# Rotary with a negative stride on VectorE, and the queries' 1/rms product on POOL as a step of its own

## The chip, the cores and the metric

The kernel runs on one core of a Trainium2 chip. Five engines work side by side, each through its own queue in order: TensorE (PE, with PEld for its weight loads), VectorE (DVE), ScalarE (ACT), GpSimd (POOL) and SyncE (SP), which issues the DMAs. They wait for one another by semaphores. The metric is the device time of one execution in microseconds (us), lower is better.

## The reference

Two layers of an encoder over 512 tokens of width 1024. Each has token heads (12 heads of 64, in 3 groups of 4, one key head for each group), 4 heads that attend to a memory of 256 tokens, an output projection, and a SwiGLU feed-forward part. Layer 0 (mixer A) is banded attention with rotary on the first 16 of a head's 64 elements; layer 1 (mixer B) is global attention in which queries and keys of each head go through an RMS norm and a two-axis rotary first. All is float32. What the change touches:

```python
def apply_rotary(x, cos, sin):
    half = x.shape[-1] // 2
    x1, x2 = xf[..., :half], xf[..., half:]
    return jnp.concatenate([x1 * c - x2 * s, x2 * c + x1 * s], axis=-1)

def mixer_b(q, k, v, qk_g, cos_r, sin_r, cos_c, sin_c):
    q = axial_rope(rms_norm(q, qk_g[0]), cos_r, sin_r, cos_c, sin_c)
    k = axial_rope(rms_norm(k, qk_g[1]), cos_r, sin_r, cos_c, sin_c)
    o = full_attention_blocks(q, k, v)
```

## The kernel before, in words

Tokens lie on the 128 partitions, in 4 tiles. A float32 matmul is made of three with a high and a low part of each operand: a *split* (L276) copies a source into its high part on ScalarE (L280) and subtracts that from the source on VectorE (L284, the low part). Splits of weights (whi, wlo), of queries (q, stored as q2), of probabilities (th, tl) all pass through these two lines.

A mixer makes keys and values first (`kv_pieces`), then the queries in four column groups c = 0 to 3 of four heads each (`q_pieces`; group 3 is the memory heads'), each for the four token tiles t. Below, *tile c.t* is group c, token tile t. A query tile is four pieces of matmul (`prod`, u = 0 to 3) into a PSUM bank with tag "acc" (two buffers). The last piece also takes the result out: ScalarE copies it to qx (L510 in layer 1, L512 in layer 0 and group 3), rotary is put on it, and it is split. Later `stage` turns the split tile on PE (L524) and ScalarE copies it to qT (L525).

`rope_b`, layer 1's rotary with the norm folded in: ScalarE squares (sq, L433); VectorE sums (ss, L434); POOL makes r = (ss/64 + eps) to the power -1/2 (L298, L299); VectorE meanwhile multiplies the two swapped halves with the sine table, one instruction each (rt, L441), x with the cosine table (L442), adds (L443), and multiplies with r (L444). `rope_a`, layer 0's, has no norm and works on 16 elements of each head (L422 to L425).

A head (`heads`) is, for each of four query blocks, a score matmul (L548, L549), its minimum on VectorE (nm, L559), the exponential on ScalarE (p, L560); then 1/denominator on VectorE (rd, L596) and four scalings of p on POOL (L599); then for each of four key blocks j a turn of the probabilities on PE (L609) into a PSUM tile with tag "t" (two buffers, each free again when th and tl have been made from it), the split, and the value matmuls (L623 with th, L624 with tl). After the last, ScalarE and VectorE add the two halves (tmp, L631; tok, L632).

What sets the order: all these steps are put on one time axis by `put` and `lay`, where one unit is one head; `PACE` has the offsets. The steps of queries for later groups so lie between the heads. PE's queue is exactly this order (the framework leaves it alone). In the other engines' queues the framework's scheduler decides when the program is built: it starts from the order in which steps are issued and moves an instruction ahead of others that it reckons to be not yet ready.

Of the kernel before, what the change touches and what calls it, by code (L numbers as in the profile page):

```python
# [23 lines left out]
NG = 3  # L24
NMH = 4
HD = 64
# [153 lines left out]
class Trunk:  # L180
# [246 lines left out]
    def rope_b(self, x, t, n, z):  # L427

        nc = self.nc
        v = nc.vector  # L430
        sq = self.core.tile([P, 4, HD], F32, tag="rt", name="sq", bufs=2)
        ss = self.small.tile([P, 4], F32, tag="ss4", name="ss4", bufs=2)
        nc.scalar.activation(sq[:, :n], x[:, :n], AF.Square)  # L433
        v.tensor_reduce(ss[:, :n], sq[:, :n], axis=AX.X, op=OP.add)  # L434
        r = self.small.tile([P, 4], F32, tag="r4", name="r4", bufs=3)
        self.rstd(r[:, :n], ss[:, :n], HD)
        tmp = self.core.tile([P, 4, HD], F32, tag="rt", name="rt", bufs=2)
        gc, gs = self.gt[:, z, 0, t], self.gt[:, z, 1, t]
        for h in range(2):
            o, i = slice(32 * h, 32 * h + 32), slice(32 - 32 * h, 64 - 32 * h)  # L440
            v.tensor_mul(tmp[:, :n, o], x[:, :n, i], gs[:, None, o].to_broadcast([P, n, 32]))  # L441
        v.tensor_mul(x[:, :n], x[:, :n], gc[:, None, :].to_broadcast([P, n, HD]))  # L442
        v.tensor_add(x[:, :n], x[:, :n], tmp[:, :n])  # L443
        v.tensor_mul(x[:, :n], x[:, :n], r[:, :n, None].to_broadcast([P, n, HD]))  # L444

    def rope(self, l, x, t, n, z):
        (self.rope_b(x, t, n, z) if l else self.rope_a(x, t, n))


    def kv_pieces(self, l):  # L450
        nc = self.nc
        self.ka = self.core.tile([P, NG, S], F32R, name="ka", tag="ka")
        self.kb = self.core.tile([P, NG, S], F32R, name="kb", tag="kb")
        self.vs = self.core.tile([P, NT, NG, P], F32R, name="vs", tag="vs")
        w = self.wkv

        def prod(t, st, u):
            self.ready(t)
            if u == 0:
                st["ps"] = self.tagged("acc" if t < 2 else "s")  # L460
            ps = st["ps"]
            for k in (2 * u, 2 * u + 1):
                c = slice((k % 2) * 384, (k % 2) * 384 + 384)
                self.mm3(ps[:, :384], self.hslice(0, k, t * P, t * P + P), self.hslice(1, k, t * P, t * P + P),
                         w[u][0][:, c], w[u][1][:, c], k == 0, k == KD - 1)
            if u == 3:
                kv = ps[:, :384].rearrange("p (z h d) -> p z h d", z=2, d=HD)
                r = self.rs[:, t:t + 1]
                self.split_scaled(self.vs[:, t, :, :HD], self.vs[:, t, :, HD:], kv[:, 1], r)
                kx = self.core.tile([P, 4, HD], F32, tag="qx", name="kx", bufs=3)  # L470
                ins = nc.scalar.activation(kx[:, :NG], kv[:, 0], AF.Copy, scale=r).ins
# [4 lines left out]
                self.rope(l, kx, t, NG, 1)  # L476
                st["k2"] = self.core.tile([P, 4, 3 * HD], F32R, tag="q2", name="k2", bufs=3)
                self.split(st["k2"][:, :NG, :HD], st["k2"][:, :NG, HD:P], kx[:, :NG])
                self.again(st["k2"][:, :NG])

        out = []
        for t in range(NT):
            st = {}
            out.append(([lambda t=t, st=st, u=u: prod(t, st, u) for u in range(4)],
                        lambda t=t, st=st: self.keys(st["k2"], self.ka, self.kb, t, NG)))
        return out

    def q_pieces(self, l, c, qTs, put, x0, lead):
# [6 lines left out]
        def prod(t, st, u):  # L495
            self.ready(t)
            if c not in qTs:
                qTs[c] = self.core.tile([P, 4, S], F32R, tag="qT", name="qT", bufs=2)
            if u == 0:
                st["ps"] = self.ps.tile([P, 512], F32, tag="acc", name="ps", bufs=2)  # L500
            ps = st["ps"]
            for k in (2 * u, 2 * u + 1):
                cs = slice((k % 4) * 256, (k % 4) * 256 + 256)
                self.mm3(ps[:, :256], self.hslice(0, k, t * P, t * P + P), self.hslice(1, k, t * P, t * P + P),
                         w[k // 4][0][:, cs], w[k // 4][1][:, cs], k == 0, k == KD - 1)
            if u == 3:
                qx = self.core.tile([P, 4, HD], F32, tag="qx", name="qx", bufs=3)
                q = ps[:, :256].rearrange("p (h d) -> p h d", d=HD)
                if l == 1 and c < 3:
                    nc.scalar.activation(qx, q, AF.Copy, scale=self.rs[:, t:t + 1])  # L510
# [17 lines left out]
        for t in range(NT):  # L528
            st = {}
            out.append(([lambda t=t, st=st, u=u: prod(t, st, u) for u in range(4)],  # L530
                        lambda t=t, st=st: stage(t, st)))
        return out


# [114 lines left out]
    def mixer(self, l, mkp, late, tokp):  # L649
# [8 lines left out]
        def put(x, f):  # L658
            bisect.insort(items, (x, next(count), f), key=lambda z: (-z[0], -z[1]))

        def lay(tiles, x0, dx, lag, due):

            for t, (prods, last) in enumerate(tiles):
# [582 lines left out]
```

## Time and profile before

| | |
|---|---|
| runs | 1124.85 us (median of 3; 1124.82 to 1125.47) |
| the profiled execution | 1125.38 us, its span 1123.6 us |
| mixer of layer 0 | about 0 to 140 us |
| mixer of layer 1 | about 560 to 745 us |
| in it, query tiles of group 0 (qx at) | 584.98 to 598.65 us |
| group 1 | 605.02 to 624.98 us |
| group 2 | 633.72 to 661.68 us |

How to read it: rows of a timeline begin with the start (us from the span's beginning) and the duration (us), then the engine, the line, the operation, output<-input with their shapes and how many instructions are merged (x4); brackets give the idle time before and what ended it. Rows of one line give the count and the shortest, middle and longest duration in ns, then the first and last start. Rows of stages give for each engine the busy time in the stage.

### The profile page before, as it was taken

The page shows a single profiled execution, that of the slowest core. Times are in us where ns is not written, and L with a number is a line of the kernel's source. Part 1 is how long each engine was busy: PE and PEld are TensorE (multiplying, and loading weights), DVE is VectorE, ACT ScalarE, POOL GpSimd, SP SyncE. Part 2 cuts the span into 40 slices and gives each one's busy share as a digit, 9 for nine tenths or more (in the row PEclk, how much of TensorE's full clock was granted, in tenths as well). Part 3 has the DMA queues.
Part 4 walks back from the last instruction along what each step waited for, and adds up shares of the span by engine and source line. Part 5 has one row for each costly group of instructions (what it writes and reads, how often), then busy time and mean ns, then how long its engine had stood idle before and what let it go on. Part 6 is the DMA issues. An engine that isn't in the chain of part 4 may idle for free.

```text
span 1123.6 us, 19533 instructions
## 1 busy us (share of the span) xinstructions
PE 1096.6 (98%) x7463; PEld 1003.6 (89%) x7463; DVE 844.3 (75%) x1431; ACT 660.8 (59%) x1343; POOL 203.8 (18%) x348
## 2 busy tenths in 40 slices
PE   8999999999999999999999999999999999999997
PEld 7889988899889989998898888878999899899985
DVE  5688885899557867885788998758996478669854
ACT  6678984666445634663467878756665255345631
POOL 5693331102000000000343543312000000000001
PEclk9999999999999999999999999999999999999999
DMA  6521015443753382325543221145136223423243
GB/s 237 194 81 47 20 57 206 169 132 114 243 180 112 112 283 76 112 79 195 179 150 113 76 76 39 38 150 188 39 113 217 65 76 114 149 62 103 85 166 112
DMA packets 38685, 139.29 MB, mean 124 GB/s; under 512 B 4416, under 2 KB 4800, under 8 KB 38464
## 3 DMA queue, kind: packets, MB, share of 16 engines
q1 hardware_dynamic: 38448, 137.91, 36.4%
q8 instruction: 58, 0.95, 0.3%
q14 instruction: 35, 0.29, 0.1%
q10 hardware_dynamic: 144, 0.14, 0.0%
HBM read 119.16 MB, written 18.87 MB: 123 GB/s over the span
## 4 chain that ended last, share of the span: by engine, by line
PE 68%; DVE 6%; ACT 3%; POOL 2%; issue 2%; DVEq 0%; POOLq 0%; ACTq 0%
PE ps L978 12%; PE ps L979 12%; PE ps L980 12%; PE ps L271 9%; PE ps L270 9%; PE ps L272 9%; PE tp L609 1%; PE o L624 1%; PE o L623 1%; PE s L548 1%; DVE nm L559 1%; PE s L549 1%; DVE wlo L284 1%; POOL r L299 1%; ACT whi L280 1%
## 5 line engine op out<-in xcount | busy, mean ns | idle before, releaser
L280 ACT ACTIVATE whi<-raw 128x1024 fp32r<-128x1024 f32 (+2 forms) x186 | 157.9, 863 | 185.2 <-PE ps L980 81.8
L284 DVE TENSOR_TENSOR wlo<-raw,whi 128x1024 fp32r<-128x1024 f32 (+2 forms) x178 | 175.9, 998 | 74.8 <-ACT whi L280 71.7
L978 PE MATMUL ps<-sf,whi 128*128 128x256 f32 x640 | 179.9, 281 | 0.2
L979 PE MATMUL ps<-sf,wlo 128*128 128x256 f32 x640 | 179.7, 281 | 0.0
L980 PE MATMUL ps<-sf,whi 128*128 128x256 f32 x640 | 179.7, 281 | 0.0
L270 PE MATMUL ps<-whi,f 128*128 128x512 f32 x352 | 137.2, 390 | 0.0
L271 PE MATMUL ps<-wlo,f 128*128 128x512 f32 x352 | 137.1, 390 | 0.0
L272 PE MATMUL ps<-whi,f 128*128 128x512 f32 x352 | 137.0, 389 | 0.0
L980 PE MATMUL ps<-a,whi 128*128 128x256 f32 x480 | 134.4, 280 | 0.0
L978 PE MATMUL ps<-a,whi 128*128 128x256 f32 x480 | 134.3, 280 | 0.0
L979 PE MATMUL ps<-a,wlo 128*128 128x256 f32 x480 | 133.8, 279 | 0.0
L978 PEld LDWEIGHTS ps<-sf,whi 128*128 128x128 f32 x640 | 121.1, 189 | 1.1 <-ACT p L984 0.6
L979 PEld LDWEIGHTS ps<-sf,wlo 128*128 128x128 f32 x640 | 121.4, 190 | 0.5
L980 PEld LDWEIGHTS ps<-sf,whi 128*128 128x128 f32 x640 | 121.4, 190 | 0.0
L308 POOL TENSOR_SCALAR e<-sso 128x1 f32<-128x1 f32 x8 | 3.4, 424 | 566.1 <-ACT junk L303 565.9
L270 PE MATMUL ps<-whi,hT 128*128 128x256 f32 (+1 forms) x320 | 98.8, 309 | 0.9 <-ACT whi L292 0.9
L271 PE MATMUL ps<-wlo,hT 128*128 128x256 f32 (+1 forms) x320 | 93.9, 294 | 2.6 <-DVE wlo L284 1.9
L599 POOL TENSOR_SCALAR p<-p,rd 128x256 f32<-128x256 f32 (+2 forms) x128 | 78.2, 630 | 99.8 <-DVE rd L596 50.3
L272 PE MATMUL ps<-whi,hT 128*128 128x256 f32 (+1 forms) x320 | 93.7, 293 | 0.0
L979 PEld LDWEIGHTS ps<-a,wlo 128*128 128x128 f32 x480 | 90.5, 188 | 0.2
L978 PEld LDWEIGHTS ps<-a,whi 128*128 128x128 f32 x480 | 90.4, 188 | 0.2
L980 PEld LDWEIGHTS ps<-a,whi 128*128 128x128 f32 x480 | 90.1, 188 | 0.0
(201 smaller groups left out, 2735.0 us busy)
## 6 DMA issues: line engine op xcount, KB each, us to landing
raw<-in_wgu_dram SPq DMA_DIRECT2D x48, 512.0 KB, 4.4
raw<-in_wd_dram SPq DMA_DIRECT2D x44, 512.0 KB, 4.4
rb<-in_wgu_dram SPq DMA_DIRECT2D x40, 512.0 KB, 3.6
raw<-in_wo_dram SPq DMA_DIRECT2D x17, 512.0 KB, 3.6
raw<-in_wq_dram SPq DMA_DIRECT2D x16, 512.0 KB, 5.0
xt<-x SPq DMA_DIRECT2D x12, 512.0 KB, 4.5
raw<-in_wm_dram SPq DMA_DIRECT2D x8, 512.0 KB, 4.3
x<-y SPq DMA_DIRECT2D x8, 512.0 KB, 3.0
```

Of the source, the lines that this page charges most:

```text
L270: mm(out, lh, rh, start=first, stop=False)
L271: mm(out, lh, rl, start=False, stop=False)
L272: mm(out, ll, rh, start=False, stop=last)
L280: nc.scalar.activation(hi, src, AF.Copy)
L284: nc.vector.tensor_sub(lo, src, hi.bitcast(F32))
L299: g.tensor_tensor(r, r, self.mhalf[:, :r.shape[1]], op=OP.pow)
L548: nc.tensor.matmul(s[:, :n], qi, hd["ka"]()[:, k0 * P:k1 * P], start=True, stop=False)
L549: nc.tensor.matmul(s[:, :n], qi, hd["kb"]()[:, k0 * P:k1 * P], start=False, stop=True)
L599: self.pooled = nc.gpsimd.tensor_scalar(hd["p"][z][:, :n], hd["p"][z][:, :n], rd[:, z:z + 1], 1.0, op0=OP.mult, op1=OP.mult)
L978: mm(out, wh[:, s], rh, start=start and k == 0, stop=False, skip_group_check=True)
L979: mm(out, wl[:, s], rh, start=False, stop=False, skip_group_check=True)
L980: mm(out, wh[:, s], rl, start=False, stop=k == 3, skip_group_check=True)
```

## The change

The two multiplications of the swapped halves become one in both ropes: x is read as (heads, 2 halves, half length) with the axis of the halves running backwards. `rope_b` no longer multiplies with r; it returns it. For keys the product follows at once, on VectorE as before. For queries the product goes to POOL, and product and split become a step of their own (`parts`), which `lay` puts 0.15 after the end of the tile's pieces (x0 + (t + 1) dx), where the split was part of the last piece (x0 + (t + 0.75) dx). In layer 0 and group 3 there is no r, and `parts` is the split alone.

```diff
+    def halves(self, x):
+        return x.rearrange("p n (h d) -> p n h d", h=2)
...
-        v.tensor_mul(tmp[:, :n, 0:8], x[:, :n, 8:16], sn[:, None, 0:8].to_broadcast([P, n, 8]))
-        v.tensor_mul(tmp[:, :n, 8:16], x[:, :n, 0:8], sn[:, None, 8:16].to_broadcast([P, n, 8]))
+        v.tensor_mul(self.halves(tmp[:, :n]), self.halves(x[:, :n, 0:16])[:, :, ::-1],
+                     self.halves(sn[:, None, :].to_broadcast([P, n, 16])))
...
-        for h in range(2):
-            o, i = slice(32 * h, 32 * h + 32), slice(32 - 32 * h, 64 - 32 * h)
-            v.tensor_mul(tmp[:, :n, o], x[:, :n, i], gs[:, None, o].to_broadcast([P, n, 32]))
+        v.tensor_mul(self.halves(tmp[:, :n]), self.halves(x[:, :n])[:, :, ::-1],
+                     self.halves(gs[:, None, :].to_broadcast([P, n, HD])))
         v.tensor_mul(x[:, :n], x[:, :n], gc[:, None, :].to_broadcast([P, n, HD]))
         v.tensor_add(x[:, :n], x[:, :n], tmp[:, :n])
-        v.tensor_mul(x[:, :n], x[:, :n], r[:, :n, None].to_broadcast([P, n, HD]))
+        return r
...
+                st["qx"], st["r"] = qx, None
                 if c < 3:
-                    self.rope(l, qx, t, 4, 0)
-                st["q2"] = self.core.tile([P, 4, 3 * HD], F32R, tag="q2", name="q2", bufs=3)
-                self.split(st["q2"][:, :, :HD], st["q2"][:, :, HD:P], qx)
+                    st["r"] = self.rope(l, qx, t, 4, 0)
+
+        def parts(st):
+            qx, r = st["qx"], st["r"]
+            if r is not None:
+                nc.gpsimd.tensor_tensor(qx, qx, r[:, :, None].to_broadcast([P, 4, HD]), op=OP.mult)
+            st["q2"] = self.core.tile([P, 4, 3 * HD], F32R, tag="q2", name="q2", bufs=3)
+            self.split(st["q2"][:, :, :HD], st["q2"][:, :, HD:P], qx)
...
+                for f in mid:
+                    put(min(x0 + (t + 1) * dx + 0.15, due(t) - 0.002), f)
```

PE's queue and SP's are the same before and after. Line numbers shift: in the rows of the changed kernel the product is L524, L437 is the sum of squares (L434 before), L442 the swapped halves (L441), L444 and L445 the cosine product and the sum (L442 and L443), L514 and L436 are qx and sq (L510 and L433), L535 is qT (L525), L569 and L570 are nm and p (L559 and L560), L606 is rd (L596), L609 the scaling of p (L599), L641 and L642 are tmp and tok (L631 and L632).

POOL's queue before, for tiles 2.0 and 2.1 (r_7950 and r_8079 are their 1/rms, ss their sums of squares, p the probabilities of the head in hand):

```order
L298 TENSOR_SCALAR r_7950<-ss_7947 128x4
L299 TENSOR_TENSOR r_7950<-r_7950,mhalf 128x4
L599 TENSOR_SCALAR p<-p,rd 128x512 x4
L298 TENSOR_SCALAR r_8079<-ss_8076 128x4
L299 TENSOR_TENSOR r_8079<-r_8079,mhalf 128x4
```

And POOL's queue in the changed kernel, from the same place (r_7922 and r_8050 belong to tiles 2.0 and 2.1):

```order
L298 TENSOR_SCALAR r_7922<-ss_7919 128x4
L299 TENSOR_TENSOR r_7922<-r_7922,mhalf 128x4
L609 TENSOR_SCALAR p<-p,rd 128x512 x4
L524 TENSOR_TENSOR qx<-qx,r_7922 128x256
L298 TENSOR_SCALAR r_8050<-ss_8047 128x4
L299 TENSOR_TENSOR r_8050<-r_8050,mhalf 128x4
L609 TENSOR_SCALAR p<-p,rd 128x512 x4
L524 TENSOR_TENSOR qx<-qx,r_8050 128x256
```

The product stands behind the four scalings. It stands so in tiles 1.1, 1.3 and 2.0 to 2.3; in group 0 and in tiles 1.0 and 1.2 it stands right behind the root.

ScalarE's queue before, around the split of tile 2.1 (q_8088 is its high part, th the high parts of turned probabilities):

```order
L510 ACTIVATE qx<-ps,rs 128x256
L433 ACTIVATE sq<-qx 128x256
L560 ACTIVATE p,den<-s,nm 128x512
L280 ACTIVATE th<-tp 128x512
L631 ACTIVATE tmp<-o 64x512
L525 ACTIVATE qT<-tp 128x4x128
L280 ACTIVATE q_8088<-qx 128x4x64
L280 ACTIVATE th<-tp 128x512
L560 ACTIVATE p,den<-s,nm 128x512
L280 ACTIVATE th<-tp 128x512
```

And in the changed kernel:

```order
L514 ACTIVATE qx<-ps,rs 128x256
L436 ACTIVATE sq<-qx 128x256
L570 ACTIVATE p,den<-s,nm 128x512
L280 ACTIVATE th<-tp 128x512
L641 ACTIVATE tmp<-o 64x512
L535 ACTIVATE qT<-tp 128x4x128
L570 ACTIVATE p,den<-s,nm 128x512
L280 ACTIVATE q_8088<-qx 128x4x64
L280 ACTIVATE th<-tp 128x512 x2
L570 ACTIVATE p,den<-s,nm 128x512
```

The split now stands one exponential later, and still ahead of both th; it waits for POOL where it waited for VectorE. In tiles 1.3 and 2.0 it stands ahead of qT and th, in tile 1.1 ahead of the next tile's qx.

VectorE's queue before, for the same tile (tl is the low part of turned probabilities):

```order
L443 TENSOR_TENSOR qx<-qx,rt 128x256
L284 TENSOR_TENSOR tl<-tp,th 128x512
L444 TENSOR_TENSOR qx<-qx,r_8079 128x256
L559 TENSOR_REDUCE nm<-s 128x1
L632 TENSOR_TENSOR tok<-o,tmp 64x512
L284 TENSOR_TENSOR q_8088<-qx,q_8088 128x4x64
L284 TENSOR_TENSOR tl<-tp,th 128x512
L559 TENSOR_REDUCE nm<-s 128x1
```

And in the changed kernel, from the swapped halves on:

```order
L442 TENSOR_TENSOR rt<-qx,gt 128x256
L437 TENSOR_REDUCE ss_8047<-sq 128x4
L444 TENSOR_TENSOR qx<-qx,gt 128x256
L606 RECIPROCAL rd<-den 128x4
L445 TENSOR_TENSOR qx<-qx,rt 128x256
L284 TENSOR_TENSOR tl<-tp,th 128x512
L569 TENSOR_REDUCE nm<-s 128x1
L642 TENSOR_TENSOR tok<-o,tmp 64x512
L569 TENSOR_REDUCE nm<-s 128x1
L284 TENSOR_TENSOR q_8088<-qx,q_8088 128x4x64
L284 TENSOR_TENSOR tl<-tp,th 128x512 x2
```

The product with r is gone from VectorE; the low part of the split stands one minimum later, ahead of two tl.

More of the change, by code (lines that the diff above doesn't have):

```diff
@@ L438, in rope_b @@
         gc, gs = self.gt[:, z, 0, t], self.gt[:, z, 1, t]
-        for h in range(2):
-            o, i = slice(32 * h, 32 * h + 32), slice(32 - 32 * h, 64 - 32 * h)
-            v.tensor_mul(tmp[:, :n, o], x[:, :n, i], gs[:, None, o].to_broadcast([P, n, 32]))
+        v.tensor_mul(self.halves(tmp[:, :n]), self.halves(x[:, :n])[:, :, ::-1],
+                     self.halves(gs[:, None, :].to_broadcast([P, n, HD])))
         v.tensor_mul(x[:, :n], x[:, :n], gc[:, None, :].to_broadcast([P, n, HD]))
         v.tensor_add(x[:, :n], x[:, :n], tmp[:, :n])
-        v.tensor_mul(x[:, :n], x[:, :n], r[:, :n, None].to_broadcast([P, n, HD]))
+        return r
     def rope(self, l, x, t, n, z):
-        (self.rope_b(x, t, n, z) if l else self.rope_a(x, t, n))
+        return self.rope_b(x, t, n, z) if l else self.rope_a(x, t, n)
     def kv_pieces(self, l):
@@ L475, in prod @@
                         nc.sync.dma_start(self.mT[:, z, ks].bitcast(F32), self.spill[:, z, ks])
-                self.rope(l, kx, t, NG, 1)
+                r = self.rope(l, kx, t, NG, 1)
+                if l:
+                    nc.vector.tensor_mul(kx[:, :NG], kx[:, :NG], r[:, :NG, None].to_broadcast([P, NG, HD]))
                 st["k2"] = self.core.tile([P, 4, 3 * HD], F32R, tag="q2", name="k2", bufs=3)
@@ L530, in q_pieces @@
             out.append(([lambda t=t, st=st, u=u: prod(t, st, u) for u in range(4)],
-                        lambda t=t, st=st: stage(t, st)))
+                        lambda t=t, st=st: stage(t, st), lambda st=st: parts(st)))
         return out
@@ L661, in lay @@
         def lay(tiles, x0, dx, lag, due):
-            for t, (prods, last) in enumerate(tiles):
+            for t, (prods, last, *mid) in enumerate(tiles):
                 for u, f in enumerate(prods):
                     put(x0 + (t + u / len(prods)) * dx, f)
+                for f in mid:
+                    put(min(x0 + (t + 1) * dx + 0.15, due(t) - 0.002), f)
                 put(min(x0 + (t + 1) * dx + lag, due(t) - 0.001), last)
```

## The prediction

> **What bounds the kernel now.** I read the page first: span, busy shares, and the shares of the chain that ended last.
>
> ```profile
> span 1123.6 us, 19533 instructions
> PE 1096.6 (98%) x7463; PEld 1003.6 (89%) x7463; DVE 844.3 (75%) x1431; ACT 660.8 (59%) x1343; POOL 203.8 (18%) x348
> PE 68%; DVE 6%; ACT 3%; POOL 2%; issue 2%; DVEq 0%; POOLq 0%; ACTq 0%
> ```
>
> TensorE is the bound: it stands still for 1123.6 - 1096.6 = 27 us. The change touches the mixers alone, so the next view is the busy time of each engine by stage: layer 1's first queries (585 to 600), its heads of groups 0 to 2 (600 to 668), and layer 0's heads.
>
> ```profile
> core 0: us, PE busy (x) PEld busy (x) DVE busy (x) ACT busy (x) POOL busy (x), PEclk, DMA share, GB/s
> 585.00:600.00 15.00, 13.14 (x98) 11.94 (x98) 11.73 (x31) 8.27 (x20) 5.14 (x7) 1.00 0.06 13
> 600.00:632.00 32.00, 31.49 (x226) 28.16 (x225) 28.06 (x65) 25.50 (x60) 16.95 (x24) 1.00 0.45 160
> 632.00:668.00 36.00, 34.48 (x235) 29.89 (x235) 34.26 (x68) 28.92 (x68) 17.76 (x24) 1.00 0.17 59
> 43.00:112.00 69.00, 66.56 (x525) 63.26 (x523) 55.61 (x172) 51.20 (x142) 41.75 (x66) 1.00 0.26 86
> ```
>
> From 632 to 668 VectorE is 95% busy (34.26 of 36) while PE idles 1.5 us; at 600 to 632 PE idles 0.5, at 585 to 600 1.9. So **all that a lighter VectorE can win in layer 1 is some 3 us**: 1.5 + 0.5 + about 1.1, the one stall at 585 to 600 that VectorE's own queue makes (quoted below). The clock is granted in full.
>
> **The change part by part.** First, prices.
>
> ```profile
> L441 DVE TENSOR_TENSOR rt<-qx,gt x24: 275/282/432, 585.5 to 663.0; 128x128 f32<-128x128 f32 x24
> L442 DVE TENSOR_TENSOR qx<-qx,gt x12: 406/418/426, 586.4 to 663.3; 128x256 f32<-128x256 f32 x12
> L444 DVE TENSOR_TENSOR qx<-qx,r x12: 408/426/885, 588.2 to 664.7; 128x256 f32<-128x256 f32 x12
> L643 POOL TENSOR_TENSOR gt<-ru x2: 734/1225/1716, 275.1 to 275.8; 128x256 f32<-128x256 f32 x2
> ...
> 275.08 2.42 POOL L643 TENSOR_TENSOR gt<-ru 128x256 f32<-128x256 f32 x2
> 275.26 1.64 DVE L284 TENSOR_TENSOR wlo<-rb,whi 128x1024 fp32r<-128x1024 f32 x1
> ```
>
> (1) **The swapped halves.** Two instructions of 0.28 become one of 256 elements. No row shows a negative stride. Lower end 0.42, as L442 with as many elements; upper end 0.84, twice that, as if it streamed at half the rate. I take 0.42, the nearest row: VectorE gains 0.14 in each of 12 tiles, and in layer 0, where such instructions are shorter still, no more. In layer 0 nothing waits on it (55.6 of 69 us busy), so I take 0 there, with 1 us either way for the splits that move. Where the sum of squares stood between the two halves, it now stands behind the whole: 0.14 later. At 0.84 it would be another 0.42 later.
>
> The Trainium skill's Vector Engine (DVE) Microarchitecture Reference, section 5.1, lists how the engine streams an operand with a negative step among the things not measured; the bounds above do without it.
>
> (2) **The product on POOL.** Twelve times 0.43 leave VectorE (0.86 where POOL scales probabilities beside it) and twelve products come to POOL. The nearest row is L643: the same engine, operation and size, one operand repeated. It took 0.73 and 1.72. I take 0.73, since the long one, from 275.8, ran beside a VectorE instruction with two operands in SBUF, and beside the new product VectorE reads PSUM or waits; 1.72 stays as the upper end. By itself it costs nothing: POOL is 18% busy.
>
> The Trainium skill's GPSIMD Engine Reference, section 3, speaks against the move: elementwise work belongs on VectorE, and it measures a two-input add at 1.96 times VectorE's time. By that the product would take 0.43 x 1.96, an estimate of 0.83, and the sum below would be 6 x 0.1 = 0.6 us higher; L643 over L444, 734 to 426, is 1.7 times.
>
> (3) **Where the product stands.** This decides. Tile 2.1 as it ran, from the timelines of POOL, ScalarE, VectorE and TensorE:
>
> ```profile
> 644.67 0.19 POOL L298 TENSOR_SCALAR r<-ss 128x4 f32<-128x4 f32 x1 [5.16 <-DVE ss L434]
> 644.95 1.17 POOL L299 TENSOR_TENSOR r<-r,mhalf 128x4 f32<-128x4 f32 x1
> 646.11 3.27 POOL L599 TENSOR_SCALAR p<-p,rd 128x512 f32<-128x512 f32 x4
> 647.11 0.42 ACT L280 ACTIVATE q<-qx 128x256 fp32r<-128x256 f32 x1
> 647.43 0.58 ACT L280 ACTIVATE th<-tp 128x512 fp32r<-128x512 f32 x1
> 646.22 0.86 DVE L444 TENSOR_TENSOR qx<-qx,r 128x256 f32<-128x256 f32 x1
> 648.75 0.67 DVE L284 TENSOR_TENSOR tl<-tp,th 128x512 fp32r<-128x512 f32 x1
> 649.48 0.66 PE L609 MATMUL tp<-cst,p 128*128 128x128 f32 x4
> ```
>
> VectorE could multiply at 646.22, as soon as POOL had the root. In the changed queue (shown with the change) the product stands behind the four scalings of the head in hand, on an engine that works in order. The scalings took 2.87 us at the least (a row below). So the product ends at 646.11 + 0.15 (late sum of squares) + 2.87 + 0.73 = 649.86, where ScalarE began the split at 647.11. The split stands in ScalarE's queue ahead of the two th, and its other half stands in VectorE's ahead of the two tl; **all behind it wait**. Then q and th: 649.86 + 0.32 + 0.58 = 650.76; tl ends 0.67 later at 651.43. The next turn of probabilities on PE (L609) needs the PSUM buffer that this tl frees: it went at 649.48 and now goes at 651.5, 2.0 us late, with PE idle before it. What follows on PE, up to the next tile's qx, is issued behind it, so the next round starts late too: the slips add.
>
> The other five tiles with the scalings between root and product, their scalings on POOL and then what waits on PE:
>
> ```profile
> 614.34 3.05 POOL L599 TENSOR_SCALAR p<-p,rd 128x512 f32<-128x512 f32 x4
> 628.31 3.23 POOL L599 TENSOR_SCALAR p<-p,rd 128x512 f32<-128x512 f32 x4
> 636.65 2.87 POOL L599 TENSOR_SCALAR p<-p,rd 128x512 f32<-128x512 f32 x4
> 655.01 2.87 POOL L599 TENSOR_SCALAR p<-p,rd 128x512 f32<-128x512 f32 x4
> 664.59 3.31 POOL L599 TENSOR_SCALAR p<-p,rd 128x512 f32<-128x512 f32 x4
> 617.53 0.36 PE L270 MATMUL ps<-whi,hT 128*128 128x256 f32 x1
> 632.29 0.40 PE L624 MATMUL o<-tl,vs 128*128 128x512 f32 x1
> 641.75 0.40 PE L624 MATMUL o<-tl,vs 128*128 128x512 f32 x1
> 658.93 0.66 PE L609 MATMUL tp<-cst,p 128*128 128x128 f32 x4 [0.63 <-DVE tl L284]
> 668.08 0.60 PE L609 MATMUL tp<-cst,p 128*128 128x128 f32 x4
> 638.99 0.59 ACT L525 ACTIVATE qT<-tp 128x512 fp32r<-128x512 f32 x1
> 639.47 0.59 ACT L280 ACTIVATE th<-tp 128x512 fp32r<-128x512 f32 x1
> 616.04 0.48 ACT L510 ACTIVATE qx<-ps,rs 128x256 f32<-128x256 f32 x1 [0.24 <-PE ps L272]
> ```
>
> - Tile 2.2: 655.01 + 0.15 + 3.60 = 658.76; q, th, tl as above (1.57): 660.33 for 658.93, **1.4**.
> - Tile 2.3: 664.59 + 0.15 + 3.60 + 1.57 = 669.91 for 668.08, **1.8**.
> - Tile 2.0: here qT stands between q and th (0.48, from 638.99 to 639.47): 636.65 + 0.15 + 3.60 + 0.32 + 0.48 + 0.58 + 0.67 = 642.45; the value product L624 waits for this tl, 641.75 before: **0.7**.
> - Tile 1.3: the same without the 0.15 (both halves stood ahead of the sum): 633.96 for 632.29, **1.7**.
> - Tile 1.1: product done at 614.34 + 3.60 = 617.94; the split stands ahead of the next tile's qx (616.04 before), which now starts at 618.26 and ends at 618.74. Its accumulator is the one that PE's L270 at 617.53 takes over: **1.2**.
>
> Tiles 1.0 and 1.2 have the product straight behind the root and the wait is short: 0. Sum with 2.0 for tile 2.1: 2.0 + 1.4 + 1.8 + 0.7 + 1.7 + 1.2 = **8.8 us**.
>
> (4) **Group 0 of layer 1**, where no head runs yet.
>
> ```profile
> 593.50 0.50 PE L524 MATMUL tp<-identr,q 128*128 128x128 f32 x4 [0.48 <-DVE q L284]
> 597.43 0.39 PE L271 MATMUL ps<-wlo,hT 128*128 128x256 f32 x1 [1.13 <-DVE wlo L284]
> ```
>
> The product is 0.73 - 0.43 longer, the merge 0.14 shorter: each of the first two splits comes some 0.2 later, and PE waits for it. Then wlo no longer queues behind a product that waits for the root, and the 1.13 goes. But tile 0.2's product now meets that wlo, and ScalarE comes late to its exponentials. I take 0, with -1 to +1.
>
> All DMA issues keep their place on SP, and PE's order is unchanged, so no transfer moves by more than these slips. After 668 nothing makes them up: PE, 98% busy over the span, is in order and carries them to the end. Sum: the profiled execution took 1125.38, its span 1123.6 and 1.8 around it; + 8.8 gives 1134.2. Against the median of the runs, 1124.85, 0.5 lower: 1133.7. **I predict 1134.**
>
> **The rivals.**
>
> *Faster: the lighter VectorE decides.* From 632 to 668 it was the fullest engine after PE, and it loses 0.86 + 0.14 a tile and the slowed half of the split. If ScalarE came to the split only after the product had ended, all 3 us of idle PE might go: 1121.8. The point from which it decides: the product must end where ScalarE reaches it, about 647.8 in tile 2.1 (one exponential, 0.7, now stands ahead of the split that began at 647.11), so 2 us earlier than reckoned. Against it: root and scalings alone end at 649.1. **0.11.**
>
> *Nothing changes: the wait replaces waits that were there.*
>
> ```profile
> 659.86 0.69 ACT L560 ACTIVATE p<-s,nm 128x512 f32<-128x512 f32 x1 [1.79 <-DVE nm L559]
> ```
>
> ScalarE idled anyway behind these instructions for VectorE's minima, here 1.8 us; if PE's buffers give as much room, the slip is 0 to 0.3 a tile: 1125 to 1127. Against it: L609 already waited for tl at 649.48 and 658.93, so there is no room. Nor does the change fail to do what it says: each tile's swap is one instruction in the new queue. **0.11.**
>
> *Slower still: the product at its upper end.* 1.72 for 0.73 adds 1.0 in six tiles, and 1 in group 0: 1141. **0.10.** The swap at 0.84 adds 6 x 0.42 = 2.5, and stays inside my forecast's own range.
>
> **How the numbers follow.** My forecast, slips of 4 to 14 us, has 0.68: 1129 to 1139. From 1124.5 to 1141 lie the forecast, the upper price and about half of "nothing", 0.83 together, so that is the range. A measurement of this kernel tells about 0.2% (2.2 us) from no change. Faster by over that 0.11, within 0.10, slower 0.79 (a slip of 0.3 a tile ends just outside).
>
> **What would show it.**
>
> ```profile
> 643.18 0.47 ACT L510 ACTIVATE qx<-ps,rs 128x256 f32<-128x256 f32 x1
> 652.10 0.46 ACT L510 ACTIVATE qx<-ps,rs 128x256 f32<-128x256 f32 x1
> ```
>
> Right: ScalarE's q waits about 2 us for POOL in six tiles of layer 1; L609 and L624 on PE idle for tl there; from one qx to the next of group 2 pass 10 to 11 us, here 8.92; VectorE's share at 632 to 668 falls while the stage grows; everything before 585 and the FFN are as long as before. Wrong: q finds its operand ready, the POOL product is over 1.5 us or the swap over 0.6, or the time moves in layer 0.

## The result, and the profile after

The changed kernel took **1134.16 us** (median of 4 executions, 1133.92 to 1134.17), the one before 1124.84 (1124.79 to 1125.47) beside it: a ratio of 1.0081, 95% interval 1.0064 to 1.0099. Put on another chip among the experiments it took 1132.99 (1.0079, 1.0065 to 1.0093). The forecast was 1134, with 1124.5 to 1141 as its range. Among the experiments one execution of the kernel before ran at a granted clock of 0.56 and took 1795 us; no comparison counts it.

The page of the profile after: the span, the busy time of each engine, and the chain that ended last.

```profile
span 1132.4 us, 19488 instructions
PE 1099.4 (97%) x7463; PEld 1005.6 (89%) x7463; DVE 834.4 (74%) x1387; ACT 660.7 (58%) x1343; POOL 207.2 (18%) x360
PE 66%; DVE 5%; POOL 3%; ACT 3%; issue 2%; DMA 1%; POOLq 0%; DVEq 0%; ACTq 0%
```

VectorE has 10 us less work than before and POOL 3 more, as the change says. TensorE's idle time grew by 6 us, to 33, and its busy time by 2.8, though it runs the same 7463 instructions. That second number needs an explanation of its own; it comes below.

The prices, from the views of the two lines (least, median and most ns of one):

```profile
L442 DVE TENSOR_TENSOR rt<-qx,gt x12: 410/416/427, 585.2 to 669.4; 128x256 f32<-128x256 f32 x12
L524 POOL TENSOR_TENSOR qx<-qx,r x12: 612/614/730, 587.7 to 674.5; 128x256 f32<-128x256 f32 x12
```

Tile 2.1, the one that the prediction worked through: POOL, ScalarE, VectorE and TensorE in turn. In square brackets is how long the engine stood idle before the row, and what ended that.

```profile
648.98 2.71 POOL L609 TENSOR_SCALAR p<-p,rd 128x512 f32<-128x512 f32 x4
651.65 0.62 POOL L524 TENSOR_TENSOR qx<-qx,r 128x256 f32<-128x256 f32 x1
652.30 0.42 ACT L280 ACTIVATE q<-qx 128x256 fp32r<-128x256 f32 x1 [2.15 <-POOL qx L524]
652.62 1.07 ACT L280 ACTIVATE th<-tp 128x512 fp32r<-128x512 f32 x2
653.23 1.29 DVE L284 TENSOR_TENSOR tl<-tp,th 128x512 fp32r<-128x512 f32 x2
654.07 0.63 PE L619 MATMUL tp<-cst,p 128*128 128x128 f32 x4 [3.28 <-DVE tl L284]
```

Read it from the bottom: PE stands for 3.28 us, until VectorE has made a tl; the tl needs a th; both th stand in ScalarE's queue behind q; q stands 2.15 us, until POOL's product is done; the product stands behind four scalings that have nothing to do with it. Two of ScalarE's instructions were ready and could not pass the one that wasn't. TensorE's other waits of that kind, from its timeline (tiles 1.1, 2.0, 2.2 and 2.3):

```profile
621.99 0.63 PE L619 MATMUL tp<-cst,p 128*128 128x128 f32 x4 [1.36 <-DVE tl L284]
...
644.69 0.51 PE L634 MATMUL o<-tl,vs 128*128 128x512 f32 x1 [0.23 <-DVE tl L284]
...
664.95 0.63 PE L619 MATMUL tp<-cst,p 128*128 128x128 f32 x4 [2.07 <-DVE tl L284]
...
676.87 0.63 PE L619 MATMUL tp<-cst,p 128*128 128x128 f32 x4 [1.52 <-DVE tl L284]
```

Tile 1.3 has no such wait, though its q stood 1.92 us for POOL. The value product that takes the low part queued behind this q (a PE instruction that multiplies tl with the values) had 1.84 us of room before. Here are the tl and the product before; then q, the tl and the product after:

```profile
631.41 0.67 DVE L284 TENSOR_TENSOR tl<-tp,th 128x512 fp32r<-128x512 f32 x1
633.92 0.40 PE L624 MATMUL o<-tl,vs 128*128 128x512 f32 x1
...
632.74 0.42 ACT L280 ACTIVATE q<-qx 128x256 fp32r<-128x256 f32 x1 [1.92 <-POOL qx L524]
634.17 0.69 DVE L284 TENSOR_TENSOR tl<-tp,th 128x512 fp32r<-128x512 f32 x1
635.10 0.39 PE L634 MATMUL o<-tl,vs 128*128 128x512 f32 x1
```

The tl ends at 634.86, 2.8 us later than before, and the product starts at 635.10, 1.2 later, as late as PE was already: the room took up the wait.

The same stage by its rhythm: the first qx of layer 1, those of group 2, and the first of group 3 (line 516).

```profile
584.08 0.46 ACT L514 ACTIVATE qx<-ps,rs 128x256 f32<-128x256 f32 x1
...
636.17 0.47 ACT L514 ACTIVATE qx<-ps,rs 128x256 f32<-128x256 f32 x1
...
645.94 0.47 ACT L514 ACTIVATE qx<-ps,rs 128x256 f32<-128x256 f32 x1
...
656.61 0.47 ACT L514 ACTIVATE qx<-ps,rs 128x256 f32<-128x256 f32 x1
...
667.91 0.47 ACT L514 ACTIVATE qx<-ps,rs 128x256 f32<-128x256 f32 x1 [0.32 <-PE ps L272]
...
679.40 0.47 ACT L516 ACTIVATE qx<-ps,rq 128x256 f32<-128x256 f32 x1
```

From one qx of group 2 to the next pass 9.8, 10.7 and 11.3 us. From 584.08 to 679.40 are 95.32 us; before, the same stretch (584.98 to 670.66) took 85.68. So the loss of 9.3 lies here, 9.64 by this measure. After it the changed kernel stays 8.3 to 8.8 us behind, up to the end. The busy time by stage says so from another side: from 632 to 676 VectorE is now busy for 31.0 us of 44 (70%, where it was 95%), and PE is idle for 6.3.

The last view is one that the prediction didn't ask for again after it had found the clock granted in full: 1 us windows, with TensorE's granted clock in the column PEclk.

```profile
core 0: us, PE busy (x) PEld busy (x) DVE busy (x) ACT busy (x) POOL busy (x), PEclk, DMA share, GB/s
666.00:667.00 1.00, 1.00 (x6) 0.87 (x5) 0.92 (x2) 0.41 (x2) 0.00 (x0) 0.65 0.06 16
667.00:668.00 1.00, 1.00 (x6) 1.00 (x5) 0.37 (x1) 0.68 (x3) 0.00 (x0) 0.50 0.00 0
668.00:669.00 1.00, 1.00 (x4) 0.71 (x4) 0.24 (x1) 0.80 (x2) 0.00 (x0) 0.50 0.45 74
669.00:670.00 1.00, 1.00 (x7) 0.80 (x6) 1.00 (x3) 0.51 (x1) 0.00 (x0) 0.65 0.93 266
```

For 3.4 us, from 666.3 to 669.7, the clock was granted at half, 1.4 us after the end of PE's second long stop. A matmul of 256 columns takes 0.42 there in place of 0.28. The price is the missing share: 0.35 + 0.50 + 0.50 + 0.35 = **1.7 us** on PE; set beside the same instructions before, PE goes into the stretch 6.02 us late and comes out 7.58 late. It explains more than half of the growth in PE's busy time. How much of it the end of the kernel keeps is reckoned below.

### The profile page after: what moved, and what is told of

The parts are those of the page before. It is cut to its first block, busy times and chain, and to the rows that moved or that the text cites. A ratio compares the mean times of both kernels' runs of the same rounds, so it can differ in the third digit from the quotient of the medians.

```text
span 1132.4 us, 19488 instructions
## 1 busy us (share of the span) xinstructions
PE 1099.4 (97%) x7463; PEld 1005.6 (89%) x7463; DVE 834.4 (74%) x1387; ACT 660.7 (58%) x1343; POOL 207.2 (18%) x360
## 4 chain that ended last, share of the span: by engine, by line
PE 66%; DVE 5%; POOL 3%; ACT 3%; issue 2%; DMA 1%; POOLq 0%; DVEq 0%; ACTq 0%
PE ps L990 12%; PE ps L992 12%; PE ps L991 12%; PE ps L271 9%; PE ps L270 9%; PE ps L272 9%; POOL p L609 1%; PE tp L619 1%; PE o L634 1%; DVE wlo L284 1%; PE o L633 1%; POOL r L299 1%; DMA pair<-whi 1%; POOL qx L524 1%; PE s L558 1%
## 5 line engine op out<-in xcount | busy, mean ns | idle before, releaser
L609 POOL TENSOR_SCALAR p<-p,rd 128x256 f32<-128x256 f32 (+2 forms) x128 | 74.4, 600 | 101.6 <-DVE rd L606 46.5
```

The source lines that it names most:

```text
L609: self.pooled = nc.gpsimd.tensor_scalar(hd["p"][z][:, :n], hd["p"][z][:, :n], rd[:, z:z + 1], 1.0, op0=OP.mult, op1=OP.mult)
```

## The experiments

Four theories were held against each other. **A**, the prediction's: the product waits behind four scalings on POOL, and the split that waits for it blocks what is queued behind it on ScalarE and VectorE. **B**: what costs is the product on POOL as such, its 0.61 us and what it takes from VectorE beside it, wherever it stands. **C**: the merged swap with its negative stride. **D**: the split's own, later step. Each run is compared with runs of the kernel before on its own chip.

### The product back on VectorE, all else as changed

```diff
-                nc.gpsimd.tensor_tensor(qx, qx, r[:, :, None].to_broadcast([P, 4, HD]), op=OP.mult)
+                nc.vector.tensor_mul(qx, qx, r[:, :, None].to_broadcast([P, 4, HD]))
```

> The changed kernel with one edit: the queries' product with 1/rms goes back from POOL to VectorE; the merged swap and the split's own step stay. Theory A (on POOL the product stands behind four scalings of 2.7 us, and the split that waits for it blocks ScalarE and VectorE): the wait goes, so 1123 to 1126 us, q on ScalarE waits under 0.3 us in the tiles of group 2, and qx to qx there is 8.9 to 9.3 us. Theory C (the merged swap with its negative stride costs the time) and theory D (the split's own later step costs it): both parts are still here, so 1132 to 1135.

Measured: **1122.52 us**, ratio 0.9984 (0.9975 to 0.9993). This is 0.5 below A's range. Tile 2.1 in its timelines, VectorE's product and ScalarE's q:

```profile
645.68 0.43 DVE L524 TENSOR_TENSOR qx<-qx,r 128x256 f32<-128x256 f32 x1 [0.27 <-POOL r L299]
646.28 0.41 ACT L280 ACTIVATE q<-qx 128x256 fp32r<-128x256 f32 x1
```

VectorE takes the product 0.03 us after the root is there; q waits for nobody, and the longest wait of PE for a tl that is left in group 2 is 0.31. The whole loss is gone, and slightly more, with merged swap and own step in place: C and D fall. (qx to qx in group 2 is 8.6 to 9.2 here.)

### The merged swap alone

The product is back on VectorE and the split back in the same step as the swap; only the merge is left. Three dots mark what is left out of an edit; here it is the rest of the step's own function, which goes.

```diff
                 if c < 3:
-                    st["r"] = self.rope(l, qx, t, 4, 0)
-
-        def parts(st):
...
+                    r = self.rope(l, qx, t, 4, 0)
+                    if r is not None:
+                        nc.vector.tensor_mul(qx, qx, r[:, :, None].to_broadcast([P, 4, HD]))
+                st["q2"] = self.core.tile([P, 4, 3 * HD], F32R, tag="q2", name="q2", bufs=3)
+                self.split(st["q2"][:, :, :HD], st["q2"][:, :, HD:P], qx)
```

> Only the merged swap is left of the change; product on VectorE and the split in the same step as before the change. Theory A: no loss, 1123.5 to 1125.5 us (the one instruction took 0.42 us for the two of 0.28, on an engine that seldom sets the pace). Theory C: 1132 to 1135. Theory D: as A here; it is told apart by the difference to the run with the product on VectorE.

Measured: **1123.34 us**, 0.9991 (0.9982 to 1.0), 0.2 below A's range. A swap of 0.42 for two of 0.28 wins at most 0.2%, and loses nothing. With the split's own step (1122.52) it is no slower.

### The product on POOL, issued early

The product goes into the step of the swap; the split keeps its own. The order of POOL's queue changes by that: in tiles 1.3 and 2.0 to 2.3 the product now comes behind the first of the four scalings, in tile 1.1 still behind all four.

```diff
                 if c < 3:
-                    st["r"] = self.rope(l, qx, t, 4, 0)
+                    r = self.rope(l, qx, t, 4, 0)
+                    if r is not None:
+                        nc.gpsimd.tensor_tensor(qx, qx, r[:, :, None].to_broadcast([P, 4, HD]), op=OP.mult)
...
         def parts(st):
             qx, r = st["qx"], st["r"]
-            if r is not None:
-                nc.gpsimd.tensor_tensor(qx, qx, r[:, :, None].to_broadcast([P, 4, HD]), op=OP.mult)
```

> The product stays on POOL but is issued in the same step as the swap, so that in tiles 1.3 and 2.0 to 2.3 it stands behind one scaling and not four; in tile 1.1 still behind four. The split keeps its step. Theory A: the product ends about 2 us earlier in those tiles, but ScalarE also comes to q about 1 us earlier (before the copy of qT and an exponential), so about 1 us of wait stays in each of the four tiles of group 2: 1127 to 1131 us, between the two kernels. Theory B (what costs is the time of a product on POOL, its own 0.61 us and what it takes from VectorE by running beside it, wherever it stands): 1133 to 1136, as all twelve products are still on POOL.

Measured: **1127.68 us**, 1.0029 (1.0018 to 1.0041). POOL, ScalarE and PE in tile 2.1 (POOL's product is line 521 here):

```profile
645.80 0.69 POOL L609 TENSOR_SCALAR p<-p,rd 128x512 f32<-128x512 f32 x1
646.46 0.61 POOL L521 TENSOR_TENSOR qx<-qx,r 128x256 f32<-128x256 f32 x1
647.11 0.42 ACT L280 ACTIVATE q<-qx 128x256 fp32r<-128x256 f32 x1 [1.31 <-POOL qx L521]
650.17 0.63 PE L619 MATMUL tp<-cst,p 128*128 128x128 f32 x4 [1.46 <-DVE tl L284]
```

The product ends 2 us sooner after the root, but ScalarE now reaches q before the copy of qT and an exponential, and stands 1.31 us for it. Between the two kernels, as A said, and not what B asked for: twelve products on POOL, of the same length, at 5 to 6 us less.

### Early product, late split

As the last one, and in layer 1 the split's step comes later, so that ScalarE has a th ahead of q.

```diff
-                    put(min(x0 + (t + 1) * dx + 0.15, due(t) - 0.002), f)
+                    put(min(x0 + (t + 1) * dx + (0.45 if l else 0.15), due(t) - 0.002), f)
```

> As the run with the early product, and in layer 1 the split's step comes later (0.45 of a head behind the tile instead of 0.15): on ScalarE q then stands behind the first of the two high parts th (group 2) or behind both (group 1). Theory A: q finds its operand ready in tiles 1.3 and 2.0 to 2.3 (wait under 0.3 us) and only tile 1.1 can wait; 1123 to 1126 us. Theory B: 1133 to 1136, as all twelve products are still on POOL. Theory D (a later split costs by itself): over 1134.

Measured: **1122.85 us**, 0.9987 (0.9978 to 0.9996), 0.15 below A's range. Tile 2.1, and the one wait of more than 0.75 us that PE has left in the stage (tile 1.1's):

```profile
645.53 0.69 POOL L609 TENSOR_SCALAR p<-p,rd 128x512 f32<-128x512 f32 x1
646.20 0.60 POOL L521 TENSOR_TENSOR qx<-qx,r 128x256 f32<-128x256 f32 x1
647.31 0.43 ACT L280 ACTIVATE q<-qx 128x256 fp32r<-128x256 f32 x1
620.78 0.63 PE L619 MATMUL tp<-cst,p 128*128 128x128 f32 x4 [1.35 <-DVE tl L284]
```

The product is done at 646.80, ScalarE takes q at 647.31 without a wait. Twelve products on POOL cost nothing where they stand well: **B falls**. What is lost in the changed kernel is lost by two places in two queues.

### Only the split later

The product stands behind four scalings as in the changed kernel; the edit is the one number of the last diff.

> The changed kernel with one number changed: in layer 1 the split's step comes 0.45 of a head behind the tile instead of 0.15. On POOL the product still stands behind four scalings in six tiles; on ScalarE q now stands behind the first high part th, ahead of the second (group 2), or behind the copy of qT and both th (group 1). Theory A (the harm is what stands behind the waiting q): the product ends as late as in the changed kernel, q waits still (1 to 1.6 us), but only the second th stands behind it: about half of the loss goes, 1127 to 1131 us. Theory B (a late product on POOL and its own time cost, whatever is queued behind): 1133 to 1134.

Measured: **1126.31 us**, 1.0015 (1.0006 to 1.0024), somewhat below the range that A gave. ScalarE and PE in tile 2.1, where POOL's product ends at 649.93:

```profile
649.97 0.42 ACT L280 ACTIVATE q<-qx 128x256 fp32r<-128x256 f32 x1 [1.65 <-POOL qx L524]
649.19 0.63 PE L619 MATMUL tp<-cst,p 128*128 128x128 f32 x4 [0.71 <-DVE tl L284]
```

ScalarE still stands for 1.65 us, but one th has passed q, and PE goes on 0.8 us *before* q even starts. Of the 10.2 us between the changed kernel and the run with VectorE's product (8.5 above the kernel before and 1.7 below it) 3.7 are left, so two thirds are gone, not half: PE stands 0.71 us in this tile where it stood 3.28, and without the long stops the clock stayed up throughout the stage (worth up to 1.7 of it). A wait is as dear as what is queued behind it.

### No product at all

In layer 1 the queries' product with 1/rms is left out.

```diff
-            if r is not None:
-                nc.gpsimd.tensor_tensor(qx, qx, r[:, :, None].to_broadcast([P, 4, HD]), op=OP.mult)
```

> The changed kernel without the queries' product with 1/rms in layer 1 (this part of the computation is left out); the root of the mean square is still taken, the four scalings and the split's own step stay. It shows what is to be had at most from taking the product off both engines. Theory A and the first step of the prediction (some 3 us in all): no wait for POOL, 1120.5 to 1123.5 us. If the split's own step cost by itself (theory D): over 1130. If the lighter VectorE gave much more than step 1 reckoned: under 1119.5.

Measured: **1119.66 us**, 0.9958 (0.9944 to 0.9971), a little below the range. ScalarE's first q of layer 1, from its timeline, and the window of group 0 (PE's busy time stands behind the length):

```profile
586.17 0.42 ACT L280 ACTIVATE q<-qx 128x256 fp32r<-128x256 f32 x1 [1.50 <-DVE qx L445]
```

```profile
584.00:600.00 16.00, 16.00 (x121) 15.00 (x121) 12.44 (x29) 9.69 (x22) 6.44 (x10) 1.00 0.33 100
```

The surplus comes from group 0: without the product no split waits for the root, q waits 1.50 us where it waited 2.38 before, and PE has no gap at all from 584 to 600, where it idled for 1.9 us from 585 to 600. So 4.7 us (1124.37 less 1119.66) is what can be won at most by taking this product off both engines; the prediction's 3 us counted VectorE's load and left out the wait for the root.

### A dose: the product twice

In groups 1 and 2 the product is issued twice, one behind the other (the queries are multiplied by 1/rms twice).

```diff
                 nc.gpsimd.tensor_tensor(qx, qx, r[:, :, None].to_broadcast([P, 4, HD]), op=OP.mult)
+                if c:
+                    nc.gpsimd.tensor_tensor(qx, qx, r[:, :, None].to_broadcast([P, 4, HD]), op=OP.mult)
```

> The changed kernel with the product issued twice in groups 1 and 2, one behind the other on POOL (the queries are multiplied by 1/rms twice): a dose of the product's price. Theory A: in tile 1.3 and in 2.0 to 2.3 the whole 0.61 us of the second one comes onto the path, 3.0 together, and up to 1 us more in tiles 1.1 and 1.2, against 1133.4 of the changed kernel: 1135.5 to 1138 us; qx to qx in group 2 grows by about 0.6. If the product's length is hidden (the scalings alone set the wait): 1133 to 1134.

Measured: **1141.72 us**, 1.015 (1.0136 to 1.0164): 3.7 us above the range that A gave. A miss in size, and a useful one. The second product's line, PE's longest wait in its timeline, and the granted clock in five windows:

```profile
L526 POOL TENSOR_TENSOR qx<-qx,r x8: 612/612/615, 608.4 to 681.2; 128x256 f32<-128x256 f32 x8
```

```profile
657.44 1.09 PE L621 MATMUL tp<-cst,p 128*128 128x128 f32 x4 [3.94 <-DVE tl L284]
```

```profile
657.00:658.00 1.00, 0.56 (x3) 0.59 (x4) 0.89 (x2) 0.72 (x3) 0.00 (x0) 0.64 0.00 0
660.00:661.00 1.00, 1.00 (x7) 0.97 (x6) 0.70 (x2) 0.78 (x2) 0.00 (x0) 0.66 0.00 0
674.00:675.00 1.00, 1.00 (x5) 0.82 (x5) 0.19 (x1) 0.76 (x2) 0.00 (x0) 0.83 0.13 25
687.00:688.00 1.00, 1.00 (x4) 0.78 (x3) 0.31 (x1) 0.72 (x2) 0.00 (x0) 0.50 0.00 0
688.00:689.00 1.00, 1.00 (x10) 0.91 (x9) 0.71 (x2) 0.59 (x1) 0.00 (x0) 1.00 0.00 0
```

The first turn of probabilities after the wait takes 1.09 us for four, where it took 0.63. Behind each of the three waits of 3.94, 2.75 and 2.71 us in group 2 the clock is halved, up to 660.7, 674.3 and 688.0 (a mean of 0.66 from 660 to 661 is half clock until 660.68). Three stretches for the changed kernel's one are some 3.3 us, which is about the miss. The other 5.4 of the 8.7 us over the changed kernel's 1133 come near the five products of 0.61 that A counted, 3.0, and a new wait of 2.15 us on ScalarE in tile 1.2, whose product now stands behind four scalings too. This is a sum, not shown by a run with the same waits and the clock kept up.

### The loss split by place

Two halves of the change, and the changed kernel itself, on one chip: the products of group 2 alone on POOL (the others on VectorE), and those of groups 0 and 1 alone.

```diff
-            if r is not None:
+            if r is not None and c == 2:
                 nc.gpsimd.tensor_tensor(qx, qx, r[:, :, None].to_broadcast([P, 4, HD]), op=OP.mult)
+            elif r is not None:
+                nc.vector.tensor_mul(qx, qx, r[:, :, None].to_broadcast([P, 4, HD]))
```

The other half has `c < 2`.

> The changed kernel with the products of groups 0 and 1 on VectorE again; those of group 2 stay on POOL, behind four scalings each. It splits the loss by place. From the traces of the changed kernel and of the run with all products on VectorE, set at the same first qx of layer 1 (584.1): up to the first qx of group 2 the changed kernel falls 2.9 us behind (636.17 against 633.30), from there to the end of group 2 another 7.6 (679.40 against 668.95), and 1.7 of those are a stretch of 3.4 us at half the granted clock (666.3 to 669.7) behind TensorE's idle time. Theory A, the slips add: 1122.5 + 7.6 = 1130 us with one such stretch, 1128.4 with none; 1127.5 to 1131. If the slips do not add, so that PE makes up in group 2 what group 1 lost: 1133.

> The other half: the products of groups 0 and 1 on POOL as in the changed kernel, those of group 2 on VectorE. Theory A: 1122.5 + 2.9 = 1125.4 us, 1124.5 to 1126.5, no stretch at half clock, qx to qx in group 2 8.6 to 9.2 us.

> The changed kernel itself, once more beside the two halves on the same chip: 1133 to 1134.5 us; by theory A the two halves' losses against the run with all products on VectorE (1122.5) add up to this one's, within 1.7 us, the price of one stretch at half clock.

Measured, against the kernel before: group 2 alone **1131.27 us**, 1.0057 (1.0045 to 1.007); groups 0 and 1 alone **1125.14**, 1.0006 (0.9997 to 1.0015); both **1132.99**, 1.0079. Group 2's time is 0.3 above A's range, the others are in theirs or at its edge. Above the run with every product on VectorE (1.7 us below the kernel before on its chip, where these stand 6.75, 0.62 and 8.47 above): 8.5, 2.3 and 10.2. The halves sum to 10.8 for 10.2: the slips add. The last 0.6 lies within what the clock scatters. Group 2's half has executions of 1130.0 (two, with a mean granted clock of 0.996 and 0.997) and of 1131.3 to 1131.6 (three; the two that were not profiled have 0.994 and 0.995), and its profile, of 1131.6, shows two stretches at half clock:

```profile
651.00:652.00 1.00, 1.00 (x4) 0.89 (x4) 0.00 (x0) 0.54 (x1) 0.00 (x0) 0.50 0.00 0
665.00:666.00 1.00, 1.00 (x6) 0.90 (x5) 0.36 (x1) 0.86 (x3) 0.00 (x0) 0.50 0.00 0
```

One stretch more over the 1130 us of an execution lowers the mean by 0.0015, so the slower ones fit two stretches and the faster ones one: 1.3 to 1.6 us for a stretch, by the same kernel's own executions. (Outside its stretches this profile has a granted clock of 0.95 throughout, and its matmuls are as long as in the changed kernel's: 281 ns in the FFN's group in both.)

### A version ahead of both

Early product, late split, and the two products of tiles 1.1 and 1.2 on VectorE.

```diff
                     r = self.rope(l, qx, t, 4, 0)
+                    if r is not None and c == 1 and t in (1, 2):
+                        nc.vector.tensor_mul(qx, qx, r[:, :, None].to_broadcast([P, 4, HD]))
+                    elif r is not None:
+                        nc.gpsimd.tensor_tensor(qx, qx, r[:, :, None].to_broadcast([P, 4, HD]), op=OP.mult)
```

> The run with the early product and the late split, with the products of tiles 1.1 and 1.2 on VectorE instead of POOL (1.1 is the one in which the product stood behind four scalings still and TensorE idled 1.35 us; 1.2 goes with it since it would otherwise be queued behind four scalings). Theory A: those 1.35 go, 1121.0 to 1122.0 us. If the scalings themselves are what that tile waits for (TensorE waits for POOL's p there for 0.34 us, before the change 0.51), little changes: 1122.4 to 1123.2.

Measured: **1121.54 us**, 0.9973 (0.9963 to 0.9984). Tile 1.1's product and q, and the window that had PE idle for 1.5 us in the kernel before:

```profile
614.48 0.45 DVE L521 TENSOR_TENSOR qx<-qx,r 128x256 f32<-128x256 f32 x1
615.61 0.42 ACT L280 ACTIVATE q<-qx 128x256 fp32r<-128x256 f32 x1
```

```profile
632.00:668.00 36.00, 36.00 (x250) 31.83 (x249) 31.26 (x63) 30.08 (x72) 19.24 (x28) 1.00 0.18 60
```

The 1.35 us of tile 1.1 are gone (1.45 between the two runs, each against the kernel before on its chip), and from 632 to 668 PE has no gap: with VectorE at 31.26 of 36 it is PE's stream alone that sets the pace there.

## Why the prediction was right, and where it was not

Step by step, the slip in each place. PE's queue is the same before and after, so its instructions can be set against each other one by one; each row has one of them, before and after.

| place | predicted | measured | PE's instruction |
|---|---|---|---|
| layer 0 | 0, -1 to +1 | -0.35 | matmul, 575.40 to 575.05 |
| group 0 | 0, -1 to +1 | +0.1 | matmul, 617.53 to 617.24 |
| tile 1.1 | 1.2 | 1.5 | turn of p, 620.82 to 621.99 |
| tile 1.3 | 1.7 | 0.0 | value product, 632.29 to 633.47 |
| tile 2.0 | 0.7 | 0.2 | turn of p, 643.62 to 645.03 |
| tile 2.1 | 2.0 | 3.2 | turn of p, 649.48 to 654.07 |
| tile 2.2 | 1.4 | 1.4 | turn of p, 658.93 to 664.95 |
| tile 2.3 | 1.8 | 2.8, about 1.0 of it clock | turn of p, 668.08 to 676.87 |
| six tiles | 8.8 | 9.1 | |

(Each entry is its row's slip less that of the row above: 4.59 - 1.41 = 3.2.)

- **The mechanism was right.** Its sign came: q stands for POOL for 2.21, 1.92, 2.14, 2.15, 1.92 and 1.37 us in the six tiles. Runs with the product on VectorE, and with product and split in better places on POOL, each lose all of it; halves of it cost their share.
- **Two of its six places were wrong.** For tiles 1.3 and 2.0 the prediction let the value products at 632.29 and 641.75 wait for a tl behind q. They take the tl of the turn before, whose th stands ahead of q on ScalarE. The tl behind q goes to the next value product, at 633.92 and 643.39, and had 1.84 and 1.69 us of room there. So tile 1.3 cost PE nothing where 1.7 was reckoned, and the product at 641.75 went to 642.26, 0.7 *less* late than PE was, since PE's wait of 0.58 at 640.57 was gone; the next value product and what follows it lost 0.9 again. In these two places the rival "nothing changes" had it right: PE's buffers gave room.
- **Part of it was paid in the next tile.** PE had room, ScalarE and VectorE had none: the qx of tile 2.0 is 2.45 us late (633.72 to 636.17) where PE is 1.2 late, that of tile 2.1 2.76 (643.18 to 645.94) where PE is 1.4 late. So tile 2.1's root and product start later than the prediction had them, and PE slips 3.2 there for 2.0. The run with group 2's products alone on POOL shows the same: tile 2.0 costs PE nothing there, and tile 2.1 costs 3.0.
- **The prices were off and cancel.** The scalings were taken at 2.87 and took 2.70 or 2.71 in five of the six tiles, once VectorE's product no longer ran beside them (in the run with the product on VectorE they took 3.11 to 3.23 in group 2); the product was taken at 0.73 and took 0.61. That is 0.28 too much in a tile. From the product's end to the turn on PE the sum had 1.57, and in tiles 2.1, 2.2 and 2.3 it took 1.80 or 1.81.
- **The clock was in no term.** PE lost 1.6 us in the stretch. An estimate of what is kept: tile 2.3's sum of squares stands on VectorE behind a minimum that waited for the score matmul at 668.10, and this one ended 1.0 us later than without the stretch (7.06 us late, where PE came in 6.02 late). So about 1.0 reaches the turn at 676.87; for the rest PE would have stood there anyway. It is worked out from the traces, not removed by an experiment: a run with the same waits and PE kept busy wasn't tried.
- **That the sum came out at 8.8 is in part luck.** Tiles 1.3 and 2.0 gave 2.2 less; tile 2.1 gave 1.2 of that back, the clock 1.0 and tile 1.1 0.3 more.
- **The merged swap** at 0.42: measured 0.416, and alone it costs nothing. Right, and the upper end of 0.84 is out.
- **The product's price** on POOL: 0.61 is below both the row taken (0.73) and the Trainium skill's figure. GPSIMD Engine Reference, section 3, has 1.96 times VectorE's time, for an add of 2048 elements a partition; here, with 256, it is 612 over 426, 1.44 times.
- **Group 0**: nothing on PE in the end, with its parts moved about. The stall of 1.13 for wlo went as foreseen; but q waits 3.01, 2.46, 1.91 and 3.04 us there for 2.38, 2.23, 1.56 and 2.53 before, and PE waits 0.71 for a split and, at 609.08, 0.85 for an exponential.
- **Layer 0** shows nothing beyond scatter: executions of the kernel before alone lie between 1123.7 and 1126.0.
- **Tile 1.1** had about the right size by another route: not the accumulator that the next qx frees but the tl behind q, as in the other tiles.
- **The rivals.** "Faster" asked for a product that ends 2 us sooner; made so, with the split after it, the kernel was 1.4 us faster than before, not 3. "Nothing changes" fell with PE's waits of 3.28 and 2.07 us, but for tiles 1.3 and 2.0. The product at its upper end never occurred.

## What to carry to other kernels

Before an operation is moved to an idle engine, find the row behind which it will stand there, and the rows that will stand behind its consumer: a share of 18% says nothing about the 2.7 us in front of it at that moment. In an engine that works in order, put what must wait as late as its own consumer allows (in tiles 1.3 to 2.3 of the changed kernel the turn of q on PE came 4.6 to 8.5 us after q) and let ready work go first. Before an instruction is said to wait, count which producer it takes from: here it was one turn off in two places, and there was room. Count idle time on TensorE twice where it fills well over half of a window of 3.4 us: once as it stands, and once for the clock behind it.

## What the runs showed of the hardware

- **Half clock behind idle time.** It isn't the length of a gap alone. In the changed kernel the clock stayed up behind a gap of 3.28 us and was halved 1.4 us after the end of one of 2.07; in the run with two products 2.75 and 2.71 were enough. Each stretch lasts 3.41 us. The three in that run end at 660.7, 674.3 and 688.0, 13.65 apart, four times 3.41: as if the chip judged fixed windows of that length, and halved the next one where PE had stood through most of the last. Two windows of the changed kernel, laid out from the stretch's start at 666.30, the first just ahead of it:

```profile
662.88:666.30 3.42, 1.35 (x9) 1.25 (x9) 1.94 (x4) 2.66 (x6) 0.27 (x1) 1.00 0.54 216
649.23:652.64 3.41, 1.56 (x12) 1.12 (x10) 1.30 (x3) 1.16 (x5) 3.04 (x5) 1.00 0.00 0
```

PE stood for 61% of the first, and for 54% of the second, which had the larger part of the gap of 3.28 and no half clock behind it. Laid out so in all 13 traces, from the first granted clock to PE's last matmul, the seven stretches each follow a window in which PE stood for 58 to 100%, and no other window has more than 54%. No experiment set out to test this. The Trainium skill, TensorE: Matmul & The Clock Gate, Part 1, has such a free-running window of 3.413 us. There a whole idle window brings half rate. By that rule none of the gaps of 2.07, 2.71 and 2.75 could halve the clock, and the traces disagree with it; with the window's length they agree, and the gap of 3.94 fits it, with a whole window idle.
- **A negative stride cost nothing** on VectorE: 0.416 us for 256 fp32 elements a partition, as the product with unit stride in the kernel before (0.418).
- **POOL's scalings and VectorE's product slow each other.** Four scalings of 128x512 took 2.87 to 3.31 us in the kernel before, where VectorE's product ran beside them, and 2.70 or 2.71 in five tiles of the changed one, without it; the product took 0.86 beside them in tile 2.1 and 0.43 at the median. It isn't the product alone: in tile 2.0 of the kernel before the low part of the split took 0.82 beside the scalings, for 0.43 in the changed one.
